# Merge gates and the GLA output projection of a decoder block as wide token-major products

## The chip, the cores and the metric

The kernel runs on one core of a Trainium2 chip. The time is the device time of one execution in microseconds (us), and the number compared is the median of several runs. The engines are PE (TensorE, matrix products), DVE (VectorE), ACT (ScalarE), POOL (GpSimd) and SP (SyncE, which here only issues DMAs); each runs its own instruction list in order and waits at semaphores for the others.

## The reference

One layer over 512 tokens and 1024 features, in float32. What matters here:

```python
hq, hk, hv, hr, ha, hatt, hgate = _split_cols(h @ w_in[i], SPLIT_SIZES)
...                                   # gated linear attention -> o, dilated attention -> o_att
o = o.reshape(B, S, GLA_V_W) * gla_gn[i] * jax.nn.silu(hr)
y_gla = o @ w_o_gla[i]                # 512x1024 @ 1024x1024
y_att = o_att @ w_o_attn[i]           # 512x512  @ 512x1024
g_gla, g_att = jnp.split(hgate, 2, axis=-1)
mix = (jax.nn.sigmoid(g_gla) * y_gla + jax.nn.sigmoid(g_att) * y_att) @ w_out[i]
x = x + mix
x = x + jnp.square(jax.nn.relu(rmsnorm(x, ln2[i]) @ w_mlp1[i])) @ w_mlp2[i]
x = x + jax.nn.sigmoid(rmsnorm(x, ln3[i]) @ w_pg[i]) * (p[i] @ w_pp[i])
```

## The kernel before

**Products.** Each float32 operand is split into a high part (`hi`, written by ACT, `split_hi` and L343 for weights) and a low part (`lo`, written by DVE, `split_lo` and L320). Each product of 128x128 with 128xN is three matrix instructions: hi·hi, hi·lo, lo·hi.

**Seven products in place of eight.** Most projections are cut into 2x2 blocks of the contraction (features) and of the rows or columns, and computed by the Strassen-Winograd scheme, whose weight operands are A11, S1 = A21+A22, S2 = S1+A11, S3 = A11+A21, A12, S4 = S2+A12, A22 (signs are in the stored weights' use) and whose activation operands are B11, T1, T2, T3, B21, B22, T4. There are two forms. `strassen` keeps the weights as the stationary operand and streams 256 columns (half of the tokens) in each instruction: 24 instructions for each of the seven stages. `wide` keeps the activations stationary and streams 512 output columns: its output is token-major (tokens on partitions), a stage takes two weight tiles of 128x1024 and 24 instructions of 512 columns. `fm` is the plain form with eight products' worth of work, features on partitions.

**Order of the projections** around the change: `gv` (wide), `oa` (o_att @ w_o_attn, plain, 96 instructions of 512 columns, results parked in HBM as `y_dram`), `r` (wide), the gates `gb0`, `gb1`, `ga0`, `ga1` (strassen, 168 instructions of 256 columns each), `og` (y_gla, plain, 8 x 24 instructions of 512 columns), `wo` (wide), `pp0`, `pp1` (p @ w_pp, 24 instructions of 512 columns each), `m1q0` to `m1q7` (strassen), the second MLP projection (wide) and `pg`.

**Weight stream.** `OPERANDS` lists all weight operands in the order of use. `fetch` walks it: for operand i it writes the low part (DVE), for i+1 the high part (ACT), for i+2 it makes the sum where one is due (`sums`, DVE, L293, L296, L302), for i+3 it issues the loads (`prepare`: SP loads 512 KB, L247; for sums one more load that accumulates, issued by POOL, L255, L299, L338). It runs two operands ahead of PE. There are 8 buffers for raw weights (`NRAW`), 5 for high parts (`NW`) and 4 for low parts.

**Side work.** `step` is called after every few matrix instructions. It takes one function from the list `later`, and at a pace in streamed columns one step of the generators in `side` (attention, GLA, `gla_out`). So the order in each engine's list is fixed when the kernel is recorded, by these lists.

**Gates to `wo`.** `gla_out` turns the GLA result from token-major to feature-major (32 transposes, L1206) and splits it into `og`'s operands. `merge` (L1296) brings the eight tiles of y_att back from HBM and multiplies them onto sigmoid(gb). After each `og` tile, DVE multiplies it onto sigmoid(ga) (L1389), adds (L1390), and small functions from `mix_even` and `mix_odd` build `wo`'s operands, feature-major throughout. `wo`'s result is added to x, and `x1_parts` transposes it (32 transposes, L1436) for the first MLP projection. `stores` prepares some sums for the second MLP projection in HBM.

Of the kernel before, what the change touches and what calls it, by code (L numbers as in the profile page):

```python
# [38 lines left out]
QUADS = ("quad", "quadt", "quadw")  # L39
# [11 lines left out]
def weight_units():  # L51
# [11 lines left out]
    def quad(name, src, col, kind="quad", chunk=0):  # L63
        for m, k in ((0, 0), (1, 0), (1, 1), (0, 1)):
            u.append((f"{name}.A{m + 1}{k + 1}", kind, src, 2 * chunk + k, col + m * (P if kind == "quad" else 256)))
# [17 lines left out]
    for j in range(4):  # L83
        u.append((f"oa.{j}", "half", "w_o_attn", 0, j * 2 * P))
    quadw("r", "w_in", (GR, GR + 512))
    for i in range(2):
        quad(f"gb{i}", "w_in", GATE + D + i * 512)
    for i in range(2):
        quad(f"ga{i}", "w_in", GATE + i * 512)
    fm("og", "w_o_gla", 0, 8)  # L90
    quadw("wo", "w_out", (0, 512))
    for j in range(2):
        u.append((f"pp{j}.0", "tm", "w_pp", 0, j * 512))
    for q in range(8):
        quad(f"m1q{q}", "w_mlp1", q * 512)
# [23 lines left out]
WBEGIN = {0: ((0, 0), "a"), 1: ((1, 1), "c"), 2: ((0, 1), "a")}  # L119
WEND = {3: ((0, 0), "b"), 4: ((1, 1), "a"), 5: ((0, 1), "c"), 6: ((1, 0), "a")}  # L120


def operand_order():

    names = []
    for name, kind, *_ in UNITS:
        if name == f"m2c{SEVEN[0]}.A11.0":
            names += [f"m2c{c}.{a}.{i}" for a, c in MLP2 for i in range(2)]
        elif name.startswith("m2c"):
            continue  # L130
        elif kind not in QUADS:
            names.append(name)
        elif name.endswith("A11"):
            names += [f"{name[:-3]}{a}" for a, _, _ in STAGES]
        elif name.endswith("A11.0"):
            names += [f"{name[:-5]}{a}.{i}" for a, _, _ in WIDE for i in range(2)]
# [17 lines left out]
def early():  # L154
    after_wide = False
    for n, i in OPERAND.items():
# [13 lines left out]
        elif what[:3] == "S3.":  # L170
            EARLY.setdefault(i - (5 if q == "wo" else 2), []).append((n, f"{q}.A11.{what[3:]}", f"{q}.A21.{what[3:]}"))
# [7 lines left out]
NU, NW, PIECE, WAYS = 68, 5, 8, 2  # L179

# [12 lines left out]
def block_kernel(ctx, tc, xT, x, ws, pT, wts, wha, wa2, vec, lnf, rel, onehot, ident_d, mask_d, out):  # L193
# [29 lines left out]
    pace, since, together = [2048], [0], [1]  # L223

    def step(columns=None):
# [4 lines left out]
        if n and since[0] >= n * pace[0]:  # L230
            since[0] = (since[0] - n * pace[0]) % pace[0]
            for _ in range(n):
                g = side.pop(0)
                if next(g, "end") != "end":
                    side.insert(min(WAYS - 1, len(side)), g)
# [14 lines left out]
    def prepare(i):  # L250

        name = OPERANDS[i]
        for n, a, b in EARLY.get(i, ()):
# [31 lines left out]

    def sums(i):
        q, _, what = OPERANDS[i].partition(".")
        if q.startswith("m2c") or (q == "wo" and what[:3] == "S4."):
# [15 lines left out]
    def split_weights(tag, i, bufs):  # L304

        t = wsp.tile([P, 1024 + PAD], F32R, tag=tag, name=tag, bufs=bufs)
        o = SHIFT if operand_kind(OPERANDS[i]) in ("quad", "quadt") else 0
# [16 lines left out]
    def fetch(upto):  # L324

        while done[0] < min(upto, len(OPERANDS) - 1):
            i = done[0] = done[0] + 1
            if i >= 0:
# [6 lines left out]
                for a, b, c in (("S1", "S2", "A11"), ("S2", "S4", "A12")):  # L335
                    if what[:3] == a + "." and (q.startswith("m2c") or (q == "wo" and a == "S2")):
# [40 lines left out]
    def tmaj(name, n, lhs, evac, tts=range(4), piece=PIECE, last=None, make=mmt):  # L377
# [5 lines left out]
        for tt in tts:  # L383
# [3 lines left out]
            if tt != last:  # L387
# [54 lines left out]
    def wide(name, xo, finish, base=None):  # L442
# [15 lines left out]
        for i, (op, xname, b) in enumerate(WIDE):  # L458
# [3 lines left out]
            for pr in range(4):  # L462
                wh, wl = weight(f"{name}.{op}.{pr // 2}")
                xh, xl = xo(xname, pr)
                r = slice((pr % 2) * 512, (pr % 2 + 1) * 512)
                mms = []
                for n in range(2):
                    c = slice(n * P, (n + 1) * P)
                    for k, (l, w) in enumerate(((xh, wh), (xl, wh), (xh, wl))):
                        mms.append((bank[b][n], l[:, c], w[:, r], fresh and not pr and not k, pr == 3 and k == 2))  # L470
                run(mms, 2 if base else 3, shared=True)
            if i in WBEGIN:
                (m, t), b = WBEGIN[i]
                later[0:0] = [begin(m, t, n, b) for n in range(2)]
            if i in WEND:
                (m, t), b = WEND[i]
                ends = [end(m, t, n, b) for n in range(2)]
                if base:
                    later[0:0] = ends
                else:  # L480
                    later.extend(ends)

# [563 lines left out]
    og, ons_ = [None] * KC, [None] * 4  # L1046
# [146 lines left out]
    def gla_out(h):  # L1193
# [8 lines left out]
        for f in range(2):  # L1202
# [6 lines left out]
            c = cv[:, C_GN + j:C_GN + j + 1]  # L1209
            hi = split_hi(pts, c)  # L1210
            yield
            og[j] = split_lo(pts, hi, c)
# [41 lines left out]
    for j in range(KC):  # L1254
        y = u32()
        S.activation(y, fm(None, oa, (j % 2) * 512, weight(f"oa.{j // 2}")), AF.Copy)
        S.dma_start(y_dram[j], y)
    rg, tb, ga = {}, [], []

    def gates(name, i, res, make):  # L1260

        new = [u32() for _ in range(4)]
        res.extend(new)

        def finish(m, t, s, ps):
            add(m, s, s, ps)
            later.append(lambda: make([4 * i + 2 * n + m for n in range(2)], [new[2 * n + m][:, halves(t)] for n in range(2)], s, t))

        strassen(f"{name}{i}", xs_op, finish, extra=lambda i: i % 3 == 2 and name == "ga" and next(spare, None))
# [13 lines left out]
    def sigmoid(js, outs, s, t):  # L1283
        for n in range(2):
            S.activation(outs[n], s[:, halves(n)], AF.Sigmoid)

    def flush():
        while later:
            later.pop(0)()

    side.extend(gla_out(h) for h in range(4))
    wide("r", xs_op, silu)
    for i in range(2):
        gates("gb", i, tb, sigmoid)

    def merge(j):  # L1296
        y = u32()
        GP.dma_start(y, y_dram[j])

        def mult():  # L1300
            V.tensor_tensor(tb[j], tb[j], y, op=OP.mult)
        return mult

    flush()
    later.extend(merge(j) for j in range(KC))
    spare = stores()
    for i in range(2):
        gates("ga", i, ga, sigmoid)
    drain()
    pace[0] = 2048  # L1310
    mix, mx = [None] * KC, {}
    msums = {name: [u32(), u32()] for name in ("T1", "T2", "T4")}
# [4 lines left out]
    def mix_half(pr, t):  # L1317

        o = halves(t)

        def hi():
            if not t:
                mix[2 * pr] = u32r(), u32r()
            S.activation(mix[2 * pr][0][:, o], tb[2 * pr][:, o], AF.Copy)

        def lo():
            h, l = mix[2 * pr]
            V.tensor_tensor(l[:, o], tb[2 * pr][:, o], h[:, o].bitcast(F32), op=OP.subtract)
# [529 lines left out]
```

## Time and profile before

| | before |
|---|---|
| median of 3 runs | 941.12 us (941.02 to 941.17) |
| profiled execution | 939.98 us, span of its instructions 938.2 us |
| PE, DVE, ACT, POOL busy | 929.3, 739.1, 563.8, 130.2 us |
| granted TensorE clock, mean | 0.997 of full |
| moved by DMA | 173.43 MB, mean 185 GB/s |

The span runs from the first to the last instruction of the profiled execution; what lies around it is 1.8 us, and the median of the runs is 1.1 us above that execution. In the profile's rows, "L357" is the line of the kernel before; nearly all matrix instructions have this line, since the helper `run` records them. The same helper line has another number in the changed kernel (L377; DVE's low parts L340, ACT's high parts L363, POOL's accumulations L273, L319, L358).

### The profile page before, as it was taken

Reading aid. Unit: us, or ns where it says so; the run is one execution under the profiler, and the core shown is the slowest. Engines: PE = TensorE matmul, PEld = TensorE weight load, DVE = VectorE, ACT = ScalarE, POOL = GpSimd, SP = SyncE. Lnnn points to the kernel's source line nnn. Section 1 sums busy time; section 2 is a strip of 40 time slices with the busy share of each in tenths; the row PEclk is TensorE's granted clock in tenths of the full one; section 3 lists DMA queues with packets and bytes.
Section 4 is the critical chain, followed back from the end, with each engine's and each line's share of the span. In section 5 each row is a group of like instructions: output and inputs, shape, how many; then the busy total and the mean of one; then the engine's idle time right before and its main releaser. Section 6 shows DMA issues by size and latency. Waiting matters only on the chain.

```text
span 938.2 us, 15155 instructions
## 1 busy us (share of the span) xinstructions
PE 929.3 (99%) x5834; PEld 838.3 (89%) x5834; DVE 739.1 (79%) x1045; ACT 563.8 (60%) x921; POOL 130.2 (14%) x173
## 2 busy tenths in 40 slices
PE   9999999999999999999999999999999999999996
PEld 8789998899998888999988879999999888888886
DVE  7698879866789579988967868777668878799764
ACT  7357546545675578876644468755556665556543
POOL 0150010030100012022111301111100111120000
PEclk9999999999999999999999999999999999999998
DMA  9474482883826556466897689987964888898302
GB/s 350 149 226 123 135 202 69 274 247 111 175 72 195 183 139 202 113 188 197 230 284 180 145 212 279 262 200 191 211 180 118 195 187 199 195 275 295 112 1 90
DMA packets 56649, 173.43 MB, mean 185 GB/s; under 512 B 7555, under 2 KB 14287, under 8 KB 56384
## 3 DMA queue, kind: packets, MB, share of 16 engines
q1 hardware_dynamic: 31488, 110.05, 33.4%
q0 software_dynamic: 21408, 57.90, 32.1%
q10 hardware_dynamic: 3680, 4.51, 1.3%
q8 instruction: 46, 0.75, 0.3%
q14 instruction: 27, 0.22, 0.1%
HBM read 164.00 MB, written 22.85 MB: 199 GB/s over the span
## 4 chain that ended last, share of the span: by engine, by line
PE 95%; DMA 2%; DVE 1%; ACT 1%; issue 1%; POOL 0%; POOLq 0%; DVEq 0%; SPq 0%; ACTq 0%
PE mmt L357 74%; PE smt L357 11%; PE mmt L616 2%; PE smt L1050 2%; DMA w<-in_wts_dram 1%; PE smt L990 1%; PE smt L913 1%; PE smt L883 0%; PE smt L1007 0%; PE smt L1006 0%; PE smt L882 0%; PE smt L996 0%; PE smt L1206 0%; PE smt L1106 0%; DMA u<-in_ws_dram 0%
## 5 line engine op out<-in xcount | busy, mean ns | idle before, releaser
L357 PE MATMUL mmt<-ur,hi 128*128 128x256 f32 (+1 forms) x2192 | 436.3, 297 | 0.0
L320 DVE TENSOR_TENSOR lo<-w,hi 128x1024 fp32r<-128x1024 f32 x260 | 316.1, 1221 | 59.7 <-PE mmt L357 33.5
L357 PEld LDWEIGHTS mmt<-ur,hi 128*128 128x128 f32 x2192 | 349.5, 189 | 11.7
L357 PE MATMUL mmt<-ur,lo 128*128 128x256 f32 (+1 forms) x1096 | 326.5, 298 | 0.0
L343 ACT ACTIVATE hi<-w 128x1024 fp32r<-128x1024 f32 x260 | 271.9, 1055 | 90.2 <-PE mmt L357 17.5
L357 PE MATMUL mmt<-hi,ur 128*128 128x512 f32 (+1 forms) x912 | 265.4, 375 | 0.0
L357 PEld LDWEIGHTS mmt<-ur,lo 128*128 128x128 f32 x1096 | 206.7, 189 | 5.6
L357 PEld LDWEIGHTS mmt<-hi,ur 128*128 128x128 f32 x912 | 164.9, 188 | 28.5
L357 PE MATMUL mmt<-lo,ur 128*128 128x512 f32 (+1 forms) x456 | 170.2, 373 | 0.0
L493 ACT ACTIVATE ur<-u 128x512 fp32r<-128x512 f32 x119 | 70.8, 626 | 62.9 <-DVE u L644 14.9
L357 PEld LDWEIGHTS mmt<-lo,ur 128*128 128x128 f32 x456 | 85.7, 188 | 15.1
L320 DVE TENSOR_TENSOR ur<-u,ur 128x512 fp32r<-128x512 f32 x118 | 77.4, 687 | 11.3 <-ACT ur L493 10.7
L357 PE MATMUL smt<-hi,ur 128*128 128x512 f32 x272 | 84.1, 390 | 0.0
L486 DVE TENSOR_TENSOR u<-u,mmt 128x512 f32<-128x512 f32 (+1 forms) x94 | 58.0, 651 | 26.7 <-PE mmt L357 26.5
L427 ACT ACTIVATE u<-mmt 128x512 f32<-128x512 f32 x72 | 42.9, 596 | 48.7 <-PE mmt L357 48.5
L255 POOL DMA_DIRECT2D w<-in_wts_dram x38 | 38.3, 1062 | 184.6 <-DMA w<-in_wts_dram 81.5
L357 PEld LDWEIGHTS smt<-hi,ur 128*128 128x128 f32 x272 | 50.8, 188 | 10.4
L299 POOL DMA_DIRECT2D w<-in_wts_dram x18 | 16.2, 898 | 273.5 <-DVE w L296 132.7
L357 PE MATMUL smt<-lo,ur 128*128 128x512 f32 x136 | 52.9, 389 | 0.0
L1532 ACT ACTIVATE u<-u 128x512 f32<-128x512 f32 x32 | 20.1, 628 | 31.0 <-DVE u L1529 30.9
L338 POOL DMA_DIRECT2D w<-in_wts_dram x18 | 16.6, 920 | 120.5 <-DVE lo L320 60.5
L357 PEld LDWEIGHTS smt<-lo,ur 128*128 128x128 f32 x136 | 25.5, 188 | 5.4
(241 smaller groups left out, 857.3 us busy)
## 6 DMA issues: line engine op xcount, KB each, us to landing
w<-in_wts_dram SPq DMA_DIRECT2D x170, 512.0 KB, 6.0
w<-in_wts_dram POOLq DMA_DIRECT2D x74, 512.0 KB, 6.6
m2c_S<-in_wts_dram SPq DMA_DIRECT2D x12, 512.0 KB, 7.3
m2c_S<-in_wts_dram POOLq DMA_DIRECT2D x12, 512.0 KB, 10.8
w<-m2c_S SPq DMA_DIRECT2D x12, 512.0 KB, 4.3
u<-in_xT_dram SPq DMA_DIRECT2D x8, 256.0 KB, 5.0
u<-in_ws_dram SPq DMA_DIRECT2D x8, 256.0 KB, 5.2
v_dram<-u ACTq DMA_DIRECT2D x8, 256.0 KB, 6.2
```

Of the source, the lines that this page charges most:

```text
L255: GP.dma_start(w, wts[UNIT[b]], accum_op=OP.add)
L299: GP.dma_start(w, wts[UNIT[f"{q}.A21"]], accum_op=OP.add)
L320: V.tensor_tensor(lo, x, hi.bitcast(F32), op=OP.subtract)
L338: GP.dma_start(w, wts[UNIT[f"{q}.{c}{what[2:]}"]], accum_op=OP.add)
L343: S.activation(hi[:, s], w[:, s], AF.Copy, scale=1.0 if c is None else c)
L357: TE.matmul(o, lhsT=l, rhs=r, start=a, stop=b, skip_group_check=shared)
L427: S.activation(sums[c], bank[b], AF.Copy, scale=-scale if c[0] else scale)
L486: V.tensor_tensor(out, s, ps, op=OP.subtract if m else OP.add)
L493: S.activation(hi, x, AF.Copy)
L616: TE.matmul(q0ps[i], lhsT=(hi, hi, lo)[j][:, c], rhs=(xh, xl, xh)[j], start=not k and not j, stop=k == KC - 1 and j == 2)
L1050: TE.matmul(o, lhsT=l[a][:, lc], rhs=r[b], start=start and i == 0, stop=stop and i == 2)
L1532: S.activation(s, s, AF.Square)
```

## The change

The gates become two `wide` projections instead of four `strassen` ones, so their sigmoids are token-major. `oa` is computed token-major too (`tmaj`). `og` becomes a `wide` projection of seven products, in the stage order `TIGHT` (A12 ahead of S2) and with the sums S2 and S4 made by accumulating loads onto the tiles of S1 and S2 once their low parts are written. Its result times gate, plus the other branch, is token-major and is transposed (`turned`, 32 transposes) into `wo`'s operands. `Parts` builds sums and splits of the activation operands for `og`, `wo` and the first MLP projection. Blocks of the contraction are contiguous halves for `og`, `wo` and the first MLP projection (`quadk`, `quadh`). `pp0` moves ahead of `wo`, `pp1` stays behind it. `merge` becomes a generator, `merges`, in `side`. `stores` starts at `v12` instead of at the gates.

```diff
-QUADS = ("quad", "quadt", "quadw")
+QUADS = ("quad", "quadh", "quadt", "quadw", "quadk")
+TIGHTS = ("og",)
+CHAINED = ("r", "gb", "ga", "og", "wo")
...
-    for i in range(2):
-        quad(f"gb{i}", "w_in", GATE + D + i * 512)
-    for i in range(2):
-        quad(f"ga{i}", "w_in", GATE + i * 512)
-    fm("og", "w_o_gla", 0, 8)
-    quadw("wo", "w_out", (0, 512))
-    for j in range(2):
-        u.append((f"pp{j}.0", "tm", "w_pp", 0, j * 512))
+    quadw("gb", "w_in", (GATE + D, GATE + D + 512))
+    quadw("ga", "w_in", (GATE, GATE + 512))
+    quadk("og", "w_o_gla", (0, 512))
+    u.append(("pp0.0", "tm", "w_pp", 0, 0))
+    quadk("wo", "w_out", (0, 512))
+    u.append(("pp1.0", "tm", "w_pp", 0, 512))
...
+TIGHT = tuple(WIDE[i] for i in (0, 1, 3, 2, 4, 5, 6))
...
     def prepare(i):
         name = OPERANDS[i]
+        if i % 3 == 0 and (OPERAND["v12.A11.0"] <= i < OPERAND["v0.A11"] or i >= OPERAND["gk.A11"]):
+            next(spare[0], None)
...
     def sums(i):
-        if q.startswith("m2c") or (q == "wo" and what[:3] == "S4."):
+        if q.startswith("m2c") or (q in CHAINED and what[:3] == "S4.") or (q in TIGHTS and what[:3] == "S2."):
             return
...
     def fetch(upto):
...
                 for a, b, c in (("S1", "S2", "A11"), ("S2", "S4", "A12")):
-                    if what[:3] == a + "." and (q.startswith("m2c") or (q == "wo" and a == "S2")):
+                    if what[:3] == a + "." and (q.startswith("m2c") or (q in CHAINED and a == "S2") or q in TIGHTS):
                         w = raw[f"{q}.{b}{what[2:]}"] = raw[OPERANDS[i]]
                         GP.dma_start(w, wts[UNIT[f"{q}.{c}{what[2:]}"]], accum_op=OP.add)
...
+    def merges():
+        ys = []
+        for i, (m, t, n) in enumerate([(m, t, n) for m, t in DONE for n in range(2)] + [(None, None, None)] * 2):
+            while m is not None and (m, t, n) not in tb:
+                yield
+            if m is not None:
+                y = u32()
+                GP.dma_start(y, y_dram[4 * m + 2 * t + n])
+                ys.append((tb[m, t, n], y))
+            yield
+            if i > 1:
+                b, y = ys.pop(0)
+                V.tensor_tensor(b, b, y, op=OP.mult)
...
+    side.extend([gla_out(0), gla_out(1), gla_out(2), gla_out(3), merges(), gops])
     wide("r", xs_op, silu)
-    for i in range(2):
-        gates("gb", i, tb, sigmoid)
...
-    for i in range(2):
-        gates("ga", i, ga, sigmoid)
...
+    wide("gb", xs_op, sigmoid(tb), extra=faster)
+    wide("ga", xs_op, sigmoid(ga), extra=room)
...
+    later.extend(lambda k=k: pt.__setitem__(k, split(pt[k])) for k in range(2))
+    wide("og", og_op, onto_mix, piece=2, first=True)
+    embed(0, smt)
...
+    wide("wo", mix_op, onto_x, base=begin_x, piece=2, first=True)
+    embed(1, mmt)
```

Three places show how instructions move. The first is POOL's list where the gates end. Before, the eight loads of y_att (`y_dram`) stand in one row, between accumulating weight loads of the gates (L299 for S3, L255 for S1):

```order
L518 TENSOR_TENSOR grs<-rv,mh 128x2
L299 DMA w<-in_wts_dram 128x1024
L1298 DMA u<-y_dram 128x512 x8
L299 DMA w<-in_wts_dram 128x1024
L269 DMA m2c_S_0_4854<-in_wts_dram 512x256
L1382 DMA u<-in_pT_dram 128x512 x2
```

Now they are in three groups, and ahead of the second and the third stands an accumulation onto S2 (L358), which waits for DVE's low part of that S2:

```order
L273 DMA w<-in_wts_dram 128x1024 x4
L1412 DMA u<-y_dram 128x512 x4
L358 DMA w<-in_wts_dram 128x1024
L1412 DMA u<-y_dram 128x512 x2
L358 DMA w<-in_wts_dram 128x1024
L1412 DMA u<-y_dram 128x512 x2
L273 DMA w<-in_wts_dram 128x1024 x4
L1487 DMA u<-in_pT_dram 128x512 x2
L358 DMA w<-in_wts_dram 128x1024 x4
```

The y loads moved behind work of DVE, and the four accumulations that end the rows are new: S2 and S4 of `og`.

The second is DVE's list at the gates (`lo` is a weight's low part, `ur` an activation's; L1301 and L1417 multiply y_att onto the gate). Before:

```order
L320 TENSOR_TENSOR lo_4735<-w_4598,hi_4669 128x1024
L1301 TENSOR_TENSOR u_4041<-u_4041,u_4715 128x512
L1301 TENSOR_TENSOR u_4042<-u_4042,u_4717 128x512
L1301 TENSOR_TENSOR u_4043<-u_4043,u_4719 128x512
L1198 TENSOR_TENSOR u_3786<-u_3786,u_3760 128x256
L1198 TENSOR_TENSOR u_3786<-u_3786,u_3765 128x256
L320 TENSOR_TENSOR lo_4771<-w_4246,hi_4737 128x1024
```

Now, in `ga` (`lo_4722` is S2's second tile, `lo_4755` and `lo_4787` are A12's two; L1264 and L674 make T1 and T2 of `og`):

```order
L340 TENSOR_TENSOR lo_4722<-w_4444,hi_4688 128x1024
L1417 TENSOR_TENSOR u_4299<-u_4299,u_4678 128x512
L340 TENSOR_TENSOR ur_4738<-u_4501,ur_4716 128x512
L1264 TENSOR_TENSOR u_4740<-u_4501,u_4503 128x512
L1417 TENSOR_TENSOR u_4382<-u_4382,u_4698 128x512
L340 TENSOR_TENSOR ur_4753<-u_4720,ur_4736 128x512
L340 TENSOR_TENSOR lo_4755<-w_4664,hi_4725 128x1024
L1417 TENSOR_TENSOR u_4389<-u_4389,u_4711 128x512
L340 TENSOR_TENSOR ur_4772<-u_4740,ur_4751 128x512
L1417 TENSOR_TENSOR u_4635<-u_4635,u_4731 128x512
L340 TENSOR_TENSOR ur_4783<-u_4572,ur_4770 128x512
L674 SCALAR_TENSOR_TENSOR u_4785<-u_4720,u_4574 128x512
```

The next instruction of this list is `lo_4787`; sums and splits for `og` and waits for y_att now stand among the low parts.

The third is PE's list where `og` ends. Before, `og` (`ur` streams) goes over into `wo` (`ur` stationary) with nothing between:

```order
L357 MATMUL mmt<-ur,hi 128x512 x2
L357 MATMUL mmt<-ur,lo 128x512
L357 MATMUL mmt<-ur,hi 128x512 x2
L357 MATMUL mmt<-ur,lo 128x512
L357 MATMUL mmt<-hi,ur 128x512 x2
```

Now `pp0` (into `smt`) follows `og`, with two groups of transposes (L1305) in it:

```order
L377 MATMUL mmt<-hi,ur 128x512 x2
L377 MATMUL mmt<-lo,ur 128x512
L377 MATMUL smt<-hi,ur 128x512
L377 MATMUL smt<-lo,ur 128x512
L377 MATMUL smt<-hi,ur 128x512 x2
L1305 MATMUL smt<-ident,u 128x128 x8
L377 MATMUL smt<-lo,ur 128x512
L377 MATMUL smt<-hi,ur 128x512 x2
L1305 MATMUL smt<-ident,u 128x128 x8
L377 MATMUL smt<-lo,ur 128x512
```

Of the 32 new transposes 8 stand in `og`, 16 here and 8 at the start of `wo`.

More of the change, by code (lines that the diff above doesn't have):

```diff
@@ L375, in fm, with tmaj @@
         return ps
-    def tmaj(name, n, lhs, evac, tts=range(4), piece=PIECE, last=None, make=mmt):
+    def tmaj(name, n, lhs, evac, tts=range(4), piece=PIECE, last=None, make=mmt, at=None):
         last = tts[-1] if last is None else last
@@ L386, in tmaj @@
                              for k in range(2 * n)])
-            if tt != last:
+            if at:
+                run(mms, piece)
+                fetch(OPERAND[f"{name}.{n - 1}"] + at[tt])
+            elif tt != last:
                 run(mms, piece)
@@ L1253, in block_kernel, with evac_oa, put @@
     y_dram = dr.tile([KC, P, T], F32, name="y_dram")
[L1254 to L1269, printed above, removed]
+    def evac_oa(j):
+        def put(tt, ps):
+            y = u32()
+            S.activation(y, ps, AF.Copy)
+            S.dma_start(y_dram[4 * j + tt], y)
+        return lambda tt, ps: later.append(lambda: put(tt, ps))
+    for j in range(2):
+        tmaj(f"oa{j}", 2, lambda k, tt: cols(oa[k], slice(tt * P, (tt + 1) * P)), evac_oa(j), at=((1, 1, 2, 2), (1, 2, 2, 3))[j])
+    rg, tb, ga = {}, {}, {}
     def silu(m, t, n, s, ps):
@@ L1372, in mix_op, with og_op, arrange @@
-    def mix_op(name, pr):
-        if name in ("B11", "T3"):
-            return cols(mix[2 * pr], halves(int(name == "T3")))
-        if name in ("B21", "B22"):
-            return cols(mix[2 * pr + 1], halves(int(name == "B22")))
-        return cols(mx[name, pr // 2], halves(pr % 2))
+    def og_op(name, pr):
+        while (name, 1) not in gparts.op:
+            step()
+        return gparts.get(name, pr)
+    def arrange(m, t, src, blk, parts, names, rests, col=None):
+        if (m, t) == (1, 1):
+            return
+        later.extend([rest] * rests[m, t] + turned(src, blk, m, t, col))
+        if t:
+            later.extend(turned(src, blk, 1, 1, col))
+        later.extend(parts.splits([(name, g) for name in names[m, t] for g in range(2)], LAG))
@@ L1483, in x1_ready @@
[L1483 to L1493 removed]
+    blk = {}
@@ L1497, in onto_x, with mix_op @@
         if n:
[L1498 to L1513 removed]
+            arrange(m, t, x2, blk, xparts, {(0, 0): ["B11"], (0, 1): ["T1", "T2"], (1, 0): ["T4", "B21", "B22", "T3"]},
+                    {(0, 0): 8, (0, 1): 7, (1, 0): 5}, C_LN2)
+    def mix_op(name, pr):
+        while (name, 1) not in mparts.op:
+            step()
+        return mparts.get(name, pr)
+    wide("wo", mix_op, onto_x, base=begin_x, piece=2, first=True)
+    embed(1, mmt)
     side.append(stats())
@@ L1519, in x1_op @@
     def x1_op(name, pr):
-        return cols(xop[name, pr // 2], halves(pr % 2))
+        while (name, 1) not in xparts.op:
+            step()
+        return xparts.get(name, pr)
     def quad(q):
```

339 lines of the change are left out of this document (168 added, 171 removed).

## The prediction

> **What bounds the kernel now.** I read the page first: busy times, the clock row and the chain that ended last.
>
> ```profile
> span 938.2 us, 15155 instructions
> PE 929.3 (99%) x5834; PEld 838.3 (89%) x5834; DVE 739.1 (79%) x1045; ACT 563.8 (60%) x921; POOL 130.2 (14%) x173
> PEclk9999999999999999999999999999999999999998
> PE 95%; DMA 2%; DVE 1%; ACT 1%; issue 1%; POOL 0%; POOLq 0%; DVEq 0%; SPq 0%; ACTq 0%
> ```
>
> PE is busy 99% of the span at full clock and carries 95% of the chain. Busy matrix rows could still hide waiting, so the list of waits comes next, for PE alone, and then the load by stage over the stretches gates, `og`, `wo` and the start of `m1q0`.
>
> ```profile
> PE smt L585 <- POOL ones L580: 1.0, 1, 1.0
> PE smt L1436 <- DVE u L486: 0.8, 2, 0.5
> 393.00:471.00 78.00, 78.00 (x662) 78.00 (x661) 66.88 (x97) 52.68 (x106) 15.82 (x21) 1.00 0.69 203
> 471.00:514.00 43.00, 43.00 (x198) 35.86 (x198) 31.88 (x53) 16.67 (x28) 6.94 (x8) 1.00 0.90 233
> 514.00:562.00 48.00, 47.25 (x220) 38.96 (x219) 35.03 (x44) 28.05 (x44) 8.95 (x10) 1.00 0.69 170
> 562.00:575.00 13.00, 13.00 (x84) 11.72 (x83) 11.29 (x16) 11.35 (x21) 1.96 (x2) 1.00 0.94 231
> ```
>
> In the whole span PE waits for others 1.8 us: 1.0 at the start, and 0.8 at the transposes after `wo`. The columns of the stretches are PE, weight loads, DVE, ACT, POOL busy, then clock and DMA share: no engine but PE is full, the clock is 1.00, and DVE has 14% to 27% free up to 562. So the time is what PE has to do, plus what new waits the other engines cause. A change that takes PE work away is worth all of it if nothing comes late.
>
> **What PE gains.** The price of an instruction is the distance between starts, not its listed duration, since they overlap. Rows of the timeline and of the chain in order of time:
>
> ```profile
> 361.73 0.63 PE L357 MATMUL mmt<-hi,ur 128*128 128x512 f32 x2
> ...
> 371.95 0.39 PE L357 MATMUL mmt<-hi,ur 128*128 128x512 f32 x1
> 463.66 4.74 PE mmt L357 x40
> ...
> 472.48 0.63 PE L357 MATMUL mmt<-ur,hi 128*128 128x512 f32 x2
> ...
> 516.01 0.62 PE L357 MATMUL mmt<-hi,ur 128*128 128x512 f32 x2
> 555.44 0.87 PE smt L1436 x8
> 562.70 0.88 PE smt L1436 x8
> L1436 PE MATMUL smt<-ident,u 128*128 128x128 f32 x32 | 4.4, 276 | 0.8 <-DVE u L486 0.8
> ```
>
> - A gate instruction of 256 columns: 40 in 4.74 us, 118.5 ns each.
> - One of 512 columns: `og` has 8 x 24 = 192 and runs from 472.48 to 516.01, 43.53 / 192 = 226.7 ns. In `gv` (wide) 45 starts lie between the first two rows, 10.22 / 45 = 227.1 ns. I take 226.7.
> - A transpose: 8 in 0.87 to 0.88 us, 109 ns, although each lists 276 ns.
>
> Gates: 4 x 168 = 672 narrow ones become 2 x 168 = 336 wide ones: 672 x 0.1185 = 79.6 against 336 x 0.2267 = 76.2, **3.5 us saved**. `og`: 192 become 7 x 24 = 168: 24 x 0.2267 = **5.4 us saved**. `oa`, `wo`, `pp0`, `pp1` and the MLP keep their counts. Transposes: 32 more, 32 x 0.109 = **3.5 us added**. Net for PE: **5.4 us less**.
>
> [...]
>
> **What the other engines get.** DVE and ACT pieces, by shape, and how closely they follow each other:
>
> ```profile
> L320 DVE TENSOR_TENSOR lo<-w,hi 128x1024 fp32r<-128x1024 f32 x260 | 316.1, 1221 | 59.7 <-PE mmt L357 33.5 <-ACT hi L343 13.8 <-issue 5.1
> 759.70 1.29 DVE L320 TENSOR_TENSOR ur<-u,ur 128x512 fp32r<-128x512 f32 x2
> 760.91 1.29 DVE L1551 TENSOR_TENSOR u<-u 128x512 f32<-128x512 f32 x2
> 771.07 2.35 DVE L320 TENSOR_TENSOR lo<-w,hi 128x1024 fp32r<-128x1024 f32 x2
> 773.34 1.29 DVE L320 TENSOR_TENSOR ur<-u,ur 128x512 fp32r<-128x512 f32 x2
> L343 ACT ACTIVATE hi<-w 128x1024 fp32r<-128x1024 f32 x260 | 271.9, 1055 | 90.2 <-PE mmt L357 17.5 <-PE smt L357 13.4 <-DVE w L302 13.4
> L427 ACT ACTIVATE u<-mmt 128x512 f32<-128x512 f32 x72 | 42.9, 596 | 48.7 <-PE mmt L357 48.5
> ```
>
> In a dense stretch DVE starts a piece of 512 every 0.605 us (1.21 / 2) and one of 1024 every 1.135 us (2.27 / 2). `og` has 14 weight tiles in place of 8, so 6 more high and low parts; its operands and `wo`'s need sums and splits that were partly absent before. I counted the recorded lists and multiplied by these distances, against PE's work there: `ga` 35.2 of 38.5 us, `og` 32.8 of 39.0, `pp0` 9.5 of 7.2, `wo` 30.3 of 40.7, `pp1` with `m1q0` 27.1 of 27.1. In sum 135 of 153 us: 88%, near the 86% (66.88 / 78) that the gates bear without a wait, but crowded at `pp0` and at `pp1` with `m1q0`. So DVE is not the bound; the question is what comes late at single places. I worked out four, PE's own order being the clock.
>
> DMA landing times, which these need:
>
> ```profile
> w<-in_wts_dram SPq DMA_DIRECT2D x170, 512.0 KB, 6.0
> u<-in_x_dram POOLq DMA_DIRECT2D x8, 256.0 KB, 13.4
> q1 hardware_dynamic: 31488, 110.05, 33.4%
> q0 software_dynamic: 21408, 57.90, 32.1%
> L1298 POOL DMA_DIRECT2D u<-y_dram x8: 543/873/889, 427.8 to 433.3; - x8
> ...
> DMA to landing us min/median/max: 5.6/6.1/7.9
> L338 POOL DMA_DIRECT2D w<-in_wts_dram x18: 876/876/1652, 527.2 to 814.5; - x18
> ...
> DMA to landing us min/median/max: 5.5/5.8/12.6
> L255 POOL DMA_DIRECT2D w<-in_wts_dram x38: 853/904/1623, 20.5 to 832.7; - x38
> ...
> DMA to landing us min/median/max: 5.5/9.0/19.6
> ```
>
> 1. *y_att in `ga`.* From `ga`'s first instruction: A11 ends after 24 x 0.2267 = 5.4. ACT then copies its two sums (2 x 0.6) and makes a high part (0.6): 7.3. DVE follows with a low part, T1 and the low part of S2's second tile: 2 x 0.6 + 1.2 = 9.7. The accumulation onto that tile takes POOL 0.9: 10.6. Only then goes the third group of y loads, landing 6.1 later: 16.7. DVE has waited in front of the product with it (L1417); behind stand a split, T2 and `lo_4787`: 3 x 0.6 + 1.2 = 19.7. PE wants that tile after 7 x 12 instructions and 4 transposes, 19.5, and its low part two instructions later, 19.9. At a landing of 7.9 it is 1.6 late; at 5.6, early. I take 0.6, between these, for the handovers that I did not count; ends 0 and 1.6.
> 2. *Chained accumulations in `og`.* S2 is loaded onto S1's tile, S4 onto S2's. From one low part to the next: landing 5.8, high 1.06, low 1.22, 8.1 us. PE uses S1's second tile 36 instructions into `og` and S2's second 78 in (both halves of its tiles come early), 42 x 0.2267 = 9.5 us. It fits with 1.4 us, plus what fetching ahead gives, one or two tiles of 2.7 us. I take 0; the ends are 0 and, at the 9.0 of L255, with no head start, 1.8.
> 3. *Transposes in `pp0`.* The second group of eight needs PSUM that ACT frees by two copies of 0.6 us; PE has three instructions (0.7) and four transposes (0.4) in between. It just fits if ACT is idle; behind one high part it is 1.06 late. I take 0.4; ends 0 and 1.1.
> 4. *`m1q0` with one `pp` as cover.* `wo`'s end, add, transposes, copies and T4 ran under two `pp` before (10.9 us), now under one. The third stage wants T4 7.2 + 5.7 = 12.9 us after `wo`: adds 1.4, four groups of copies and the splits on ACT until 10.4, low parts by 12.1. PE's 0.8 us wait of before goes; I put 0.4 for this one; ends 0 and 1.7, the latter if DVE runs at the listed 1.22 and 0.69.
>
> Hidden, with its cover: the six more tiles of `og` (DVE 6.8, ACT 6.3 us) under `og` itself, which has 7 us free on DVE; the earlier `stores` (24 DMAs, moved in SP's and POOL's lists past the loads of `v12` to `gb`) under PE's products, since the fetch is two tiles ahead; their place in `ga`, `og` and the MLP becomes free. DMAs: the count of recorded loads is 6 more by SP and 14 more by POOL. By share and size q1 costs 2.85 us of all 16 engines per MB (33.4% of 938.2 / 110.05), q0 5.2. `og`'s 10 loads and 8 accumulations of 0.524 MB come to 15 + 22 = 37 us in 38: full, and a reason not to take landing times at their least.
>
> **Sum**, on the profiled execution (939.98): -5.4 - 0.8 + 0.6 + 0.4 + 0.4 = -4.8, 935.2. The median of the runs stands 1.1 above that execution: **936.3 us**.
>
> **The rivals.**
> - *The gain is eaten by small waits* (same). If places 1 to 4 all come at their far ends, 1.6 + 1.8 + 1.1 + 1.7 = 6.2: -5.4 - 0.8 + 6.2 = 0.0, 941.1. For it: DVE's crowded list, the DMA load in `og`. Against: PE has never waited at such places (0.8 us in all), although a DVE load of 86% and landings of 12.6 occur. Chance 0.12.
> - *Transposes at their listed time* (same): 32 x 0.276 = 8.8 us, which is all that gates and `og` save (8.9); with the waits of above 941.1 - 0.1 - 0.8 + 1.4 = 941.6. The Trainium skill, "TensorE: Matmul & The Clock Gate", section "Part 4: PE-mode transpose", says that one takes about 275 ns in a kernel and does not keep the fast clock engaged. The duration agrees with the 276 here, the distance of 109 and the clock of 1.00 at 514 to 562 do not. Chance 0.04.
> - *Late accumulations* (slower). The x loads, accumulating too, land in 13.4 us. `og` has two links of place 2, one after the other on the same tiles; each us beyond about 9 stops PE once in each. From 12.3 us on, 2 x 3.3 = 6.6 eats gain and margin (4.8 + 1.9 to be slower); at 13.4 the time is 936.3 + 8.8 = 945. For it: 37 of 38 us of DMA work. Against: L338's median 5.8, and `stores`, which load the same stretch now, are gone from it. Chance 0.09.
>
> **How the numbers follow.** A measurement here can tell about 0.2%, 1.9 us. The forecast, waits of up to 4 us in all, spans 934.9 (no wait: 941.1 - 6.2) to 938.9 and has 0.75; it is faster. The two same-rivals have 0.16, the slower one 0.09. The range goes to 940.6, into the first rival, so that no more than 2 in 10 lie outside.
>
> **What would show it.** Gates: starts 227 ns apart, 38 us for each of `gb` and `ga` (plus their GLA work); `og` in 38 to 40 us; transposes of `mix` 8 in 0.9 us. Waits of PE: DVE low parts in `ga`, at A12's second tile, under 2 us; in `og` for S2's second tile, none; ACT at `pp0`'s transposes. The prediction is wrong if PE's own waits exceed 4 us in sum, if the wide gates do not run at 227 ns, or if PE loses time in stages that were not touched, where earlier `stores` load the DMA engines.

## The result, and the profile after

| | before | after |
|---|---|---|
| median of 12 runs each | 941.07 us | 944.18 us |
| lowest to highest | 940.06 to 943.05 | 942.92 to 945.92 |
| profiled execution | 939.98, span 938.2 | 944.67, span 942.9 |

The ratio is 1.0028, 95% interval 1.0019 to 1.0038: slower by 0.28%, where 936.3 us (0.5% faster) was forecast. The page of the changed kernel, its rows for the span, PE, the granted clock and the chain that ended last:

```profile
span 942.9 us, 14591 instructions
PE 928.4 (98%) x5506; PEld 822.4 (87%) x5506; DVE 745.9 (79%) x1049; ACT 581.3 (62%) x939; POOL 142.3 (15%) x187
PEclk9999999999999999999989999999999999999999
PE 90%; DMA 4%; ACT 2%; DVE 2%; issue 1%; POOL 0%; POOLq 0%; DVEq 0%; SPq 0%; ACTq 0%
```

One slice in the middle of the clock row reads 8 where there was a 9, and DMA has 4% of the chain in place of 2%. The list of waits, for PE alone, names what is new:

```profile
PE mmt L377 <- DVE lo L340: 4.9, 1, 4.9
PE smt L1130 <- DVE u L1110: 0.7, 1, 0.7
PE smt L1080 <- DVE ur L1143: 0.5, 1, 0.5
```

One single wait of 4.9 us. The chain of work in order of time (start, length, what) shows where it comes from:

```profile
456.06 2.57 PE mmt L377 x11
...
458.64 8.57 DMA w<-in_wts_dram
...
467.77 0.76 POOL w L273
...
469.03 0.54 POOL w L273
469.56 11.51 DMA u<-in_pT_dram
...
481.09 0.64 ACT ur L523
...
484.85 1.15 DVE lo L340
...
486.05 4.21 PE mmt L377 x9
```

A weight tile lands at 467.2; only then can POOL issue two accumulations onto such tiles (L273), and only behind these stand, in POOL's list, the two loads of `pT`, the operand of `pp0` (L1487). They land 11.5 us after issue. ACT has their high parts (L523) in its list at the start of `og`, waits for them 6.7 us, and everything behind on ACT and DVE waits too, among it the low part of a weight tile of `og`. PE's timeline there:

```profile
480.56 0.61 PE L377 MATMUL mmt<-hi,ur 128*128 128x512 f32 x2
486.05 0.80 PE L377 MATMUL mmt<-lo,ur 128*128 128x512 f32 x1 [4.87 <-DVE lo L340]
486.64 1.06 PE L377 MATMUL mmt<-hi,ur 128*128 128x512 f32 x2
...
490.48 1.05 PE L377 MATMUL smt<-hi,ur 128*128 128x512 f32 x2
...
491.59 0.63 PE L377 MATMUL smt<-hi,ur 128*128 128x512 f32 x2
```

The instruction due at 480.56 + 2 x 0.2267 = 481.0 starts at 486.05: 5.0 us late. Behind it ten starts take 4.43 us (486.05 to 490.48) in place of 2.27, and three more 1.11 in place of 0.68: 2.6 us more, because the granted clock is halved. The stretch 488 to 490 (PE, weight loads, DVE, ACT, POOL busy, clock, DMA share, GB/s):

```profile
488.00:490.00 2.00, 2.00 (x6) 1.59 (x5) 1.99 (x2) 0.72 (x1) 0.00 (x0) 0.50 0.98 129
```

So 7.6 us are lost at one place. (It is `og`'s second S1 tile: from 486.05 it is ten instructions to `smt`, the bank of the third stage, so 38 of 48 lie before. The expectations below call it the second A11 tile; that was miscounted.)

### The profile page after: what moved, and what is told of

Same layout as the page of the kernel before. It is cut to its first block, busy times and chain, and to the rows that moved or that the text cites. A ratio compares the mean times of both kernels' runs of the same rounds, so it can differ in the third digit from the quotient of the medians.

```text
span 942.9 us, 14591 instructions
## 1 busy us (share of the span) xinstructions
PE 928.4 (98%) x5506; PEld 822.4 (87%) x5506; DVE 745.9 (79%) x1049; ACT 581.3 (62%) x939; POOL 142.3 (15%) x187
## 4 chain that ended last, share of the span: by engine, by line
PE 90%; DMA 4%; ACT 2%; DVE 2%; issue 1%; POOL 0%; POOLq 0%; DVEq 0%; SPq 0%; ACTq 0%
PE mmt L377 68%; PE smt L377 13%; PE mmt L646 2%; DMA y_dram<-u 2%; PE smt L1080 1%; DMA u<-in_pT_dram 1%; DMA w<-in_wts_dram 1%; PE smt L1305 1%; PE smt L1020 1%; PE smt L943 1%; PE smt L913 0%; PE smt L1037 0%; PE smt L1036 0%; PE smt L912 0%; PE smt L1026 0%
## 5 line engine op out<-in xcount | busy, mean ns | idle before, releaser
L377 PE MATMUL mmt<-hi,ur 128*128 128x512 f32 (+1 forms) x1264 | 376.8, 381 | 0.0
L377 PE MATMUL mmt<-ur,hi 128*128 128x256 f32 (+1 forms) x1552 | 294.7, 290 | 0.0
L377 PEld LDWEIGHTS mmt<-hi,ur 128*128 128x128 f32 x1264 | 230.5, 189 | 41.3
L377 PEld LDWEIGHTS mmt<-ur,hi 128*128 128x128 f32 x1552 | 244.3, 189 | 4.2
L377 PE MATMUL mmt<-lo,ur 128*128 128x512 f32 (+1 forms) x632 | 240.3, 380 | 4.9 <-DVE lo L340 4.9
L377 PE MATMUL mmt<-ur,lo 128*128 128x256 f32 (+1 forms) x776 | 225.8, 291 | 0.0
L377 PEld LDWEIGHTS mmt<-ur,lo 128*128 128x128 f32 x776 | 146.5, 189 | 1.9
L377 PEld LDWEIGHTS mmt<-lo,ur 128*128 128x128 f32 x632 | 119.3, 189 | 27.8 <-DVE lo L340 5.6
L523 ACT ACTIVATE ur<-u 128x512 fp32r<-128x512 f32 x137 | 80.9, 626 | 61.9 <-DVE u L665 12.5
L377 PE MATMUL smt<-hi,ur 128*128 128x512 f32 x320 | 99.5, 392 | 0.0
L273 POOL DMA_DIRECT2D w<-in_wts_dram x46 | 46.0, 1073 | 220.8 <-DMA w<-in_wts_dram 92.7
L358 POOL DMA_DIRECT2D w<-in_wts_dram x28 | 25.0, 893 | 179.0 <-DVE lo L340 89.7
L319 POOL DMA_DIRECT2D w<-in_wts_dram x14 | 12.5, 894 | 212.3 <-DVE w L316 113.4
```

What stands on the lines that cost most here:

```text
L273: GP.dma_start(w, wts[UNIT[b]], accum_op=OP.add)
L319: GP.dma_start(w, wts[UNIT[f"{q}.A21"]], accum_op=OP.add)
L358: GP.dma_start(w, wts[UNIT[f"{q}.{c}{what[2:]}"]], accum_op=OP.add)
L377: TE.matmul(o, lhsT=l, rhs=r, start=a, stop=b, skip_group_check=shared)
L523: S.activation(hi, x, AF.Copy)
```

## Experiments

All are timed against the kernel before on the same chip. Its median there stood between 940.5 and 940.9, so beside each median stands the distance to it; for the changed kernel that is +3.1 us.

**Was it the loads of `pT`?** Three edits of the changed kernel, and one of the clock. `pt_early` moves these lines ahead of `ga`:

```diff
+    for k in range(2):                       # ahead of wide("ga", ...)
+        t = u32()
+        GP.dma_start(t, pT[k * P:(k + 1) * P, :])
+        pt.append(t)
```

> Only the two loads of pT move: they are issued ahead of ga, so that on POOL they stand ahead of the y loads and of the accumulations that wait for DVE; their splits stay at the start of og. Theory 1 (ACT's splits of pT, which wait 6.7 us for loads that were issued late, hold up the low part of og's second A11 tile; PE loses 5.0 us waiting and 2.6 us at half clock behind it): the wait of 4.9 us is gone, and the time is 944.2 - 7.6 = 936.6. Theory 2 (the DMA engines are full from 460 to 482, so og's own tiles would be late too, whatever pT does): another wait of 2 to 5 us takes its place in og, time 941 to 944. Theory 3 (the earlier stores delay everything on POOL and in the DMA engines): as theory 2, with pT itself late at its new place.

Measured 940.51 us (-0.3), ratio 0.9996 (0.9985 to 1.0007). The wait in `og` is gone, and another has come in `ga`. PE's timeline there:

```profile
455.57 0.50 PE L377 MATMUL smt<-lo,ur 128*128 128x512 f32 x1 [2.73 <-DVE lo L340]
```

And the stretch behind it, clock before DMA share:

```profile
458.00:460.00 2.00, 2.00 (x6) 1.62 (x5) 2.00 (x3) 0.85 (x1) 0.75 (x1) 0.50 0.43 76
```

This is place 1 of the prediction (`ga`'s second A12 tile, behind y_att), now 2.7 us, and half clock too.

`split_late` leaves the loads and moves the splits behind `og`'s second stage (`extra=pt_splits`, which appends them to `later` at i == 1).

> Only the splits of pT move: behind og's second stage, as before the change; the loads stay where the change has them, behind the accumulations. Theory 1: the loads may land at 481 and nobody on ACT or DVE stands behind them at that time, so 936.6 as with early loads; the two variants agree within 0.5 us. Theory 2: the loads still share the full DMA engines with og's tiles, and PE waits 2 to 5 us for a low part in og with no pT in its chain: 941 to 944. If it is the late landing itself that matters and not the order on ACT, this kernel stays at 944.

943.78 us (+3.0), ratio 1.0029 (1.0018 to 1.0039): no gain, against theory 1 as I had put it. In PE's list of waits no long one is left, but several shorter ones; the longest besides the 1.0 at the start:

```profile
PE mmt L377 <- ACT u L475: 1.8, 1, 1.8
PE smt L1130 <- DVE u L1110: 1.0, 1, 1.0
...
PE smt L377 <- DVE lo L340: 1.0, 1, 1.0
PE mmt L377 <- DVE lo L340: 0.7, 1, 0.7
```

The last comes from the splits at their new place. The accumulation behind that low part lands at 488.15, and ACT starts the high part at 488.25; but in DVE's list `pT`'s two splits now stand ahead of the low part and wait for their high parts, which in ACT's list stand behind two copies (L475). The low part starts at 492.05. It releases the next accumulation onto a tile of `og` (place 2), which lands 7.4 us after issue, and for that one PE waits the 1.8 us. So here too `pT`'s splits hold up a low part of `og`, only another one.

`stores_back` puts the steps of `stores` back into `ga`, `og` and the MLP.

> The sums in HBM for the second MLP projection are made at their old places again (four steps in ga, seven in og, the rest in the MLP); all else as changed. Theory 1: the stores are not the cause; more DMAs in ga and og make pT land later, so the wait at og's second A11 tile stays or grows: 944 to 948. Theory 3 (early stores are the loss): the wait shrinks, and the waits of about 0.8 and 0.7 us at 333 and 385 us go: 936 to 940.

952.24 us (+11.4), ratio 1.0119 (1.0104 to 1.0133): 8 us worse than the changed kernel. The early stores are not the cause; they are what keeps this change from being 1.2% slower. (The wait at 333 us did go, see `order_spread`.)

`filler` adds 20 useless matrix instructions to stage A11 of `og`. They stand 24 instructions ahead of the late low part, not directly ahead as the expectation says.

> As changed, and PE gets 20 matrix instructions of 512 columns into an unused bank (20 x 0.2267 = 4.5 us of useless work) just ahead of the instruction that waits for the low part. The wait for that part is not touched. Theory 1 with the clock: PE is busy through most of the wait, the granted clock stays at 1.00 behind it, and the 2.6 us of half speed go: 941.6. If the clock costs nothing there (the longer distances behind the wait are the queue refilling): 944.2 again, or up to 0.3 more.

942.86 us (+2.1), ratio 1.0026 (1.0014 to 1.0038). PE no longer stops in `og` for that part and its clock stays at 1.00, but a part of what this saves goes to the next accumulation (0.7 us for ACT L475), and y_att was late in this execution (1.2 us). So the clock follows the stop; what it costs is not separated here.

**Order or amount?** `order_only` issues `pT` ahead of `gb` and all eight y loads in one row, when `merges` starts; no DMA is added or left out. `ga_dve` leaves the order around `pT` and takes two accumulations of 0.5 MB away (`CHAINED` without `"ga"`). `v1` is both; `v3` is `v1` with the late splits.

```diff
+        for m, t in DONE:                    # at the start of merges
+            for n in range(2):
+                got[m, t, n] = u32()
+                GP.dma_start(got[m, t, n], y_dram[4 * m + 2 * t + n])
-                y = u32()
-                GP.dma_start(y, y_dram[4 * m + 2 * t + n])
-                ys.append((tb[m, t, n], y))
+                ys.append((tb[m, t, n], got[m, t, n]))
```

> Only POOL's order changes, no DMA is added or left out: the two loads of pT are issued ahead of gb, and all eight loads of y_att stand in one row ahead of ga's two accumulations onto S4 (L358), as they stood in one row before the change. Theory A (order: loads late because they are queued behind accumulations that wait for DVE): both waits go, the one at ga's second A12 tile (2.9 us with early pT) and the one at og's second A11 tile (5.0), each with its half clock; 936 to 937. Theory B (the DMA engines are the limit: their share is 0.95 to 1.0 from 420 to 480 where it was 0.55 to 0.9 before, and y lands 8 to 9 us after issue where it took 6.1): the loads are issued in time but the bytes are the same, and a wait of 2 us or more stays at one of the two places or at a weight tile: 940 to 942.

936.20 us (-4.3; 935.98 to 936.61), ratio 0.9955 (0.9944 to 0.9967). PE's waits beyond the 1.0 at the start are 0.5 and 0.2, both far ahead of `ga`. Its span is 934.2 us, and the chain of work is PE's alone from `ga` to the MLP:

```profile
434.78 14.99 PE mmt L377 x66
449.78 5.44 PE smt L377 x24
455.22 27.20 PE mmt L377 x120
482.42 5.44 PE smt L377 x24
487.86 7.26 PE mmt L377 x32
495.11 0.87 PE smt L1305 x8
495.99 14.55 PE mmt L377 x64
510.54 0.91 PE smt L377 x4
```

> ga's S4 is summed by DVE again (1.1 us twice) instead of by two accumulating loads of 0.5 MB; this also takes the two accumulations out from between the y loads. pT's loads and splits stay as changed. Theory A: the wait at ga's second A12 tile is under 0.5 us, but pT still stands behind the accumulations for og and the wait of 3 to 5 us at og's second A11 tile stays with its half clock: 941 to 944. Theory B: with 1 MB less on the POOL queue (5.5 us of all 16 engines at the page's share for q0) pT lands 3 us or more earlier and the wait falls under 2 us: 937 to 939.

943.87 us (+3.3), ratio 1.0037 (1.0025 to 1.0049). With less to move, `pT` lands 11.3 us after issue, and PE's wait is not shorter but longer:

```profile
PE mmt L377 <- DVE lo L340: 6.2, 1, 6.2
```

Theory B falls: it is the order. The DMA share (next to last column) of the stretch 420 to 460 agrees. Before:

```profile
420.00:460.00 40.00, 40.00 (x342) 40.00 (x341) 34.39 (x48) 24.32 (x43) 9.28 (x14) 1.00 0.67 189
```

After:

```profile
420.00:460.00 40.00, 40.00 (x186) 32.67 (x185) 34.18 (x47) 27.80 (x45) 9.68 (x14) 1.00 0.96 251
```

And in `order_only`, which has no wait there:

```profile
420.00:460.00 40.00, 40.00 (x187) 33.14 (x187) 35.04 (x48) 29.12 (x46) 9.55 (x14) 1.00 0.99 274
```

Landing times grew with the share: the y loads' median went from 6.1 to 8.3 us, `pT`'s from 6.7 to 11.4. Whether anybody waits is a matter of what was issued early.

> order_only and ga_dve together: y and pT early, and ga's S4 summed by DVE. Theory A: no more than order_only, 936 to 937. Theory B: 1 to 4 us below order_only, 936 to 937, since it is the lighter load that removes the rest. Both: PE waits under 2 us between 440 and 500, no half clock there. If neither holds, DVE, which gets 2.3 us more in ga, is late itself: a wait for a low part in ga without any DMA in its chain, 939 to 941.

937.67 us (-2.9; 935.37 to 940.47), ratio 0.9971 (0.9960 to 0.9983). By the distances that is 1.4 us over `order_only`, but the intervals of the two ratios overlap. The profiled execution, at 940.29 one of the longest, shows 2.0 us of waiting in `og` for ACT L475, behind accumulations that go out 2.6 to 5.3 us later than in `order_only`.

> v1 with pT's splits behind og's second stage too, as before the change, so that ACT and DVE have 2 x 1.2 us less at og's start. Theories A and B: as v1, 936 to 937, at most 0.5 us less. If the crowding of DVE and ACT at the start of og matters, 1 us or more below v1.

942.90 us (+2.4), ratio 1.0023 (1.0013 to 1.0034): 5 us worse than `v1`. PE waits in `v3` for a low part that is made from an accumulation onto an S1 tile of `og`:

```profile
PE mmt L377 <- DVE lo L340: 3.2, 1, 3.2
```

By the chains of work that accumulation lands at 488.7, in `v1` at 487.8, and ACT's high part follows at once in both. DVE starts the low part at 488.97 in `v1`, but at 492.61 in `v3`, since the moved splits stand ahead of it and wait for ACT:

```profile
490.74 1.15 ACT L523 ACTIVATE ur<-u 128x512 fp32r<-128x512 f32 x2
...
491.40 1.29 DVE L340 TENSOR_TENSOR ur<-u,ur 128x512 fp32r<-128x512 f32 x2 [4.10 <-ACT ur L523]
492.61 2.35 DVE L340 TENSOR_TENSOR lo<-w,hi 128x1024 fp32r<-128x1024 f32 x2
```

Of the 3.6 us, 0.9 are the landing and 2.7 the order on DVE. So the place that was harmless before the change is not harmless in the new `og`, and this is what `split_late` met too.

**The two halves of `order_only`, and the stores again.**

> Half of order_only: pT's two loads ahead of gb, the y loads in three groups as changed. If pT is the one loss and the three y groups cost the 0.6 us of the prediction: 936.2 to 937.0. If the y groups cost what they cost with pT loaded ahead of ga (a wait of 2.7 us and half clock behind it): 939 to 940.5, with the wait at ga's second A12 tile.

> The other half: all eight y loads in one row ahead of the accumulations, pT as changed. Theory A: the wait at og's second A11 tile stays at 3 to 5 us with its half clock, and the time is 942 to 944. If earlier y alone moves DVE and so the accumulations ahead of pT, pT lands earlier and the time comes to 938 to 940.

Early `pT` alone: 937.75 us (-2.8), ratio 0.9959 (0.9945 to 0.9973), with 0.8 us of waiting at place 1. The y row alone: 940.86 (+0.3), ratio 0.9995 (0.9983 to 1.0006). There POOL reaches `pT` 2.35 us sooner, at 467.21, and the two loads land 9.8 and 10.6 us after issue. PE's wait for them, in an execution of 939.47 us:

```profile
PE mmt L377 <- DVE lo L340: 1.4, 1, 1.4
```

The stretch around it:

```profile
482.00:484.00 2.00, 1.22 (x5) 1.05 (x6) 2.00 (x3) 2.00 (x4) 0.74 (x1) 1.00 0.00 0
```

PE stops 1.4 us, and the clock stays at 1.00. Against the changed kernel, by the distances, `pT` alone is worth 5.9 us, the y row alone 2.8, both 7.4. What the y row adds to early `pT` is not clear of noise in the ratios (0.9959 and 0.9955); in the profiled executions `ga` takes 39.9 us with early `pT` alone and 38.55 with both.

`order_stores` is `order_only` with the stores at their old places.

> order_only with the stores at their old places (ga, og, MLP). With the change's order of loads this edit alone cost 8 us. If the stores only made the late pT later, they cost under 1 us here: 936 to 937. If 24 more DMAs in ga and og make the accumulating loads of og late by themselves (rival of the prediction, late accumulations): 940 to 946, with PE waiting for low parts of og's S2 tiles or for ACT's L473.

940.88 us (+0.3), ratio 0.9995 (0.9985 to 1.0005): 4.6 us more than `order_only`. This is the prediction's third rival, late accumulations, made real: the one issued at 471.9 onto a tile of `og` lands 14.6 us later. PE's waits, with ACT's high parts (here L361) and low parts (L338):

```profile
PE mmt L375 <- ACT hi L361: 1.6, 2, 1.3
PE mmt L375 <- ACT u L473: 1.1, 1, 1.1
PE mmt L375 <- DVE lo L338: 1.1, 2, 0.5
```

`order_spread` takes the stores out of `oa`, with this set of operands in place of every third:

```diff
+SPARE = set(range(30, 44, 2)) | set(range(57, 73, 2)) | set(range(84, 111, 3))
```

> order_only with the stores' steps taken out of gv's end and oa (where the results of oa go to HBM, landing in 7 to 10 us, and DVE at 330 waits for a buffer of theirs) and made denser ahead of it. If the early stores cost the wait of PE at 332 (0.3 to 1.2 us in the kernels with them, none in before and with the stores back): that wait goes, 935.3 to 936.0, the best of all. If that wait comes from the order of the buffers alone: 936.2 again.

936.01 us (-4.6), ratio 0.9941 (0.9927 to 0.9954). The wait for L1110 is no longer listed, but the time is that of `order_only` within the intervals. These two are the fastest versions, faster than before and after.

**What a stop costs.** Four kernels on `order_only`: after the second stage of `m1q3`, where nothing is late, PE transposes a tile, POOL writes it 0, 3, 6 or 9 times, PE transposes it again.

```diff
+                TE.transpose(bank[:, 0:P], zero[0][:, 0:P], ident)
+                for _ in range(6):
+                    GP.memset(zero[0], 0.0)
+                TE.transpose(bank[:, P:2 * P], zero[0][:, 0:P], ident)
```

> order_only with two transposes of a tile of zeros after the second stage of m1q3, and nothing between them: the control for the next three. Both theories: 936.2 to 936.5 (two transposes, 0.2 us).

> As stop_0, and between the two transposes POOL writes the tile three times (0.53 us each by the page), so PE stands still for 1.6 to 1.9 us, where it had no waits before and the clock was 1.00. Theory C (a stop of PE above some length between 2.0 and 2.7 us costs half clock behind it; stops of 1.8 and 1.4 in split_late and yall kept 1.00): +1.7 and no more, clock 1.00 behind it, 938.0. Rival D (the half clock behind long waits comes from other things at those places, weight loads or the DMA): +1.7 as well.

> Six writes, a stop of 3.2 to 3.5 us. Theory C: +3.3 and 1.3 to 2.6 more by half clock for 2.6 to 5.3 us behind it (instructions of 256 columns 0.21 us apart in place of 0.118): 940.8 to 942.2. Rival D: +3.3 alone, 939.6. Rival E (while PE stands the others run ahead, which refunds part): less than 939.6.

> Nine writes, a stop of 4.8 to 5.1 us, as long as the one that the change met. Theory C: +4.9 and 2.0 to 2.6 more: 943.1 to 943.8, so the half clock was about a third of what the wait cost. Rival D: 941.2. Rival E: less than 941.2.

Over the control the medians (936.41; 936.76, 941.10, 942.99) are 0.35, 4.7 and 6.6 us longer; the first of these is within the spread of the executions (935.96 to 937.09 against 936.62 to 937.89). In the profiled executions the first MLP projection alone, from its first product to the next projection's, takes 161.5 us in the control and 1.0, 5.0 and 5.75 us more with three, six and nine writes. PE's wait and the next 792 instructions, to the end of the first MLP projection, in the chain of work. The control:

```profile
632.38 95.04 PE mmt L377 x792
```

Three writes:

```profile
PE smt L1594 <- POOL zero L1593: 1.8, 1, 1.8
```

```profile
633.91 94.00 PE mmt L377 x792
```

Six writes, with the stretch behind the stop:

```profile
PE smt L1594 <- POOL zero L1593: 3.6, 1, 3.6
```

```profile
635.94 96.15 PE mmt L377 x792
```

```profile
638.00:640.00 2.00, 2.00 (x11) 2.00 (x10) 0.00 (x0) 0.00 (x0) 0.00 (x0) 0.50 0.96 176
```

Nine writes:

```profile
PE smt L1594 <- POOL zero L1593: 5.3, 1, 5.3
```

```profile
638.12 95.12 PE mmt L377 x792
```

A stop of 1.8 us keeps the clock, and the 792 instructions then take 1.0 us less than in the control: a refund, as rival E has it, but from PE itself. PE's starts show how: 24 instructions take 2.880 us in the control, and 2.84 to 2.86 behind the stop in all three kernels, to the end of the projection. So the refund depends on how many such instructions follow.

Behind 3.6 us the clock is halved, and the 792 take 96.15 - 94.00 = 2.2 us more than behind the short stop; behind 5.3 us 1.1 more. The traces' clock records say why the longer stop costs less of it: with six writes the clock is at half for 5.2 us after PE has resumed, with nine for 2.9. The sums, 3.6 + 2.2 - 1.0 = 4.8 and 5.3 + 1.1 - 1.0 = 5.4, come within 0.4 us of the projection's 5.0 and 5.75. Rival D falls, since nothing else was late here. Theory C holds for the long stops, with half clock costing 1 to 2 us, and was wrong on the short one, where it expected the full 1.7.

## Why the prediction was wrong

**The step that failed** is the list of places in "What the other engines get": four places, and the loads and splits of `pT` are not among them. Before, the loads went out at 457.4, landed in 6.6 to 6.9 us, and the splits stood behind `og`'s second column. The change put the splits at `og`'s start, and POOL's list, which stood in the order shown ahead of the prediction, has the loads behind four L273. The two answers needed were in sight: what ACT has in its list at `og`'s start, and when POOL reaches L1487. This step cost 5.0 us of waiting and 2.6 of half clock in the profiled execution. The half clock is a second thing that the prediction put at nothing: it priced each wait at its length. Early `pT` alone brings 937.75 us, with the y row 936.2, where 936.3 was forecast. That these two stand so close is in part luck, as the next paragraphs show.

**The terms.** The lengths of the stages, in us between PE's starts in the three traces:

| | before | changed | `order_only` |
|---|---|---|---|
| up to the first product of `run` | 27.60 | 28.42 | 28.23 |
| `oa` | 25.20 | 26.06 | 25.57 |
| gates, with the GLA work among them | 92.37 | 90.57 | 90.27 |
| `og` | 43.53 | 46.67 | 39.00 |
| `pp0`, `wo`, `pp1` | 53.77 | 55.26 | 55.25 |

All other stages agree within 0.13 us. In `order_only` `og` has the forecast 39.0 us, with its 8 transposes in 0.87, and PE's wait after `wo` is gone. The gates' term was too large: 3.5 us forecast, 2.1 measured. Wide gates do start 14.99 / 66 = 227 ns apart where nothing stands between them, but over the stage the products went from 80.6 to 77.6 us only (the narrow ones, 118.5 ns in the prediction's row, took 119.9 on average there), and 60 instructions of the GLA (L1050, now L1080) got 0.9 us dearer, 0.5 of it the wait for L1143. Against before, `order_only` gains 4.3 us by medians and 4.0 by the profiled executions, where 4.8 was forecast: the 1.4 us of places 1, 3 and 4 did not come, and about as much less was saved at the gates. The kernel before, too, took 0.5 us less in the session of `order_only` (940.53).

**The places, one by one.** Place 1 (y_att; 0.6, ends 0 to 1.6): no listed wait in the changed kernel (its `ga` takes 0.36 us more than that of `order_only`), 0.8 us in `pt_gb`, 1.0 in `split_late`, 1.2 in `filler`, 2.7 plus half clock in `pt_early`, 3.5 plus half clock in `stores_back`. Its far end was too low, since it took y's landing at 6.1 to 7.9 us, from before. With the DMA share at 0.96 the y loads (L1412) of the changed kernel landed like this:

```profile
DMA to landing us min/median/max: 6.1/8.3/11.4
```

Place 2 (chained accumulations; 0): none in the changed kernel, `order_only` and `pt_gb`, but 2.0 us in `v1` and 3.8 in `order_stores`. The margin held where it was forecast, and is thin. Places 3 and 4 (0.4 each): none.

**The DMA load** was worked out for `og` alone (37 of 38 us). From 420 to 460, in the gates, where the y loads are issued, the share rose from 0.67 to 0.96, and the landing times of before were used there.

**Stores.** "Hidden under PE's products" held: early they cost, as far as `order_spread` tells, no more than the wait at 333 us, late 4.6 to 8 us. The condition in which the prediction would be wrong, PE's own waits above 4 us, is the one that came true.

**The sum.** Between the predicted 935.2 and the profiled 944.67 lie 9.5 us. By the table: 7.7 at `og`, 3.1 longer than before where 4.6 less was forecast; 1.1 at the gates, 1.8 less where 2.9 less was forecast with place 1; 0.9 in `oa`, 0.7 of it the wait for L1110; 0.8 ahead of the first product of `run`; 1.1 to the other side at `pp0`, `wo` and `pp1`, 1.5 more where 2.6 more was forecast; 0.1 in the rest. The 0.8 is not shown to be the change's: that start lies between 27.55 and 29.22 us in the profiled executions of all the kernels here.

**Readings.** The 45 starts that the prediction places in `gv` (361.73 to 371.95) lie in `r`, which is wide too and runs from 332.0 to 380.1; the price is the same. Where it says that no engine but PE is full, its own row has the weight loads of the gates at 78.00 of 78.00 us; no run here tests what that means for the narrow instructions.

**The rivals.** Each named a mechanism that was not the one: small waits added up, transposes at 276 ns, late accumulations. The third came nearest, a late DMA behind DVE's low parts on POOL's list, but it was looked for at weight tiles. Against the second, the clock of 1.00 at 514 to 562 says less than it was taken for: groups of eight transposes there last 0.9 us, so no long run of them was seen. Their distance of 109 ns does decide it.

## What to carry to other kernels

When a change moves the consumer of a load, write down for that load three things: what stands ahead of it in the issuing queue, what that waits for, and what stands behind the consumer on its engine; a load that nobody hurried before needs this as much as those that the diff speaks of. Landing times are to be taken at the DMA share of the new stretch, not of the old one. Loads that need nothing but a free buffer are best issued ahead of those that wait for another engine: here that alone turned 0.3% slower into 0.45% faster.

## What the runs showed of the hardware

Not expected: the price of a wait of PE is not its length. By the length of the projection in which they stood, a stop of 1.8 us cost 1.0 and one of 3.6 cost 5.0, because 792 instructions of 256 columns behind the short stop ran 1.0 us faster, and behind the long one the clock was halved.

Stops of up to 1.8 us left the clock at 1.00 (`yall`, `split_late`, `stop_3`); those of 2.7 us and more halved it (`pt_early`, `v3`, `stores_back`, `ga_dve`, the changed kernel, `stop_6`, `stop_9`), and so did one of 1.87 us in `stores_back`, at 508.8 to 510.7. The stretch behind that one:

```profile
512.00:514.00 2.00, 2.00 (x6) 1.41 (x6) 0.06 (x1) 1.15 (x2) 0.00 (x0) 0.50 1.13 273
```

When the clock changes is not the stop's doing alone. In the traces' clock records all changes within a run, once the clock is up, lie a whole number of 3.413 us apart, and half clock lasts one or two such pieces (3.4 us in `pt_early`, `v3` and `stop_9`, 6.8 in the changed kernel, `ga_dve` and `stop_6`). Laying this grid over PE's stops, the clock fell at the end of pieces in which PE had stood for 1.87 us (`stores_back`), 1.97 (`stop_6`), 2.00 (`pt_early`) or more, and not after 1.75 in one piece (`split_late`); the 1.81 of `stop_3` fell into two, 1.18 and 0.63. Whether the whole stop counts or its part in one piece, these runs do not separate. The Trainium skill, "TensorE: Matmul & The Clock Gate", section "Part 1: The HAM clock gate (the "warmup" mystery)", puts the fall to half rate after an idle window of about 3.4 us: the length of the pieces agrees, but 1.87 us of standing within one, with PE at work for the rest, was enough here. Why instructions follow each other more closely after a stop no run here tells.
